# Zeros on TensorE during the first loads, and the first loads spread over three queues

## The chip, the cores and the metric

The kernel runs on one core of a Trainium2 chip. The metric is the device time of one execution in microseconds, the median of several runs. The profile is one execution of the same program under the hardware profiler.

## The reference

The kernel computes two layers of a decoder trunk over 256 tokens of 1024 features in float32. Each layer is a half-step SwiGLU FFN, a gated token-mixing block (a Mamba-2 SSD mixer and a latent attention mixer side by side), and a second half-step FFN. The start of the program, where the change lies, is the first FFN:

```
h = x
for l in range(DEPTH):
    h = h + 0.5 * swiglu(rms_norm(h, ln_ffn1[l]), ffn1_w13[l], ffn1_w2[l])
    u = rms_norm(h, ln_mix[l])
    ...
    h = h + merged @ w_o[l]
    h = h + 0.5 * swiglu(rms_norm(h, ln_ffn2[l]), ffn2_w13[l], ffn2_w2[l])

def swiglu(x, w13, w2):
    gu = x @ w13
    gate, up = gu[..., :D_FF], gu[..., D_FF:]
    return (jax.nn.silu(gate) * up) @ w2
```

D_FF is 2816.

## The kernel before

Activations lie with features on the partitions: `hT` holds x as eight tiles of 128 features x 256 tokens. Products are made in two float32r parts of each factor. `operand` (L197) makes the two parts of a feature tile: ScalarE writes the high part with the gain of the norm, VectorE the low part (L203, L204). The tile `X` then has 512 columns, high and low.

The weights stream from HBM. `plan` (L79) lists every block in the order of its use; a block is 128 x 1024 floats (512 KB), and the first four are half as wide (256 KB). `ahead` (L143) issues a block's DMA from SyncE into one of four staging buffers `st` (L148), casts its high part on ScalarE (`wh`, L151) and subtracts to get its low part on VectorE (`wl`, L152); the parts have four buffers each. `mm2` (L172) multiplies a weight tile: a matmul of 512 columns with the high weights (L177) and one of 256 columns with the low ones (L178). In the text these two are a pair; a full block is eight pairs.

In `ffn` (L378), for each of 22 feature tiles i, a gate and an up product of eight pairs each go to a PSUM tile `g` (four buffers). `halves` (L180) adds the two column halves of such a tile into `t2` (two buffers, shown as `t` in the trace): a copy on ScalarE (L181), an addition on VectorE (L182). Then comes the multiplication by the row factor `Rb` of the norm (L398), silu (L400) and the product (L401). The first FFN's `Rb` is made while the first products run: squares of x on ScalarE and their sum on VectorE (L229 to L233), a sum over partitions on TensorE (L240), `rsqrt` on VectorE (L215 to L223), a broadcast on TensorE (L255), and the copy (L260). The tables for the rotary embedding and copies of constants (`tables`, L288, with `identb` at L291) are written by VectorE between these.

`consts` (L264) starts the loads. All go out from SyncE, in this order: the norm gains `vec[0][:, :24]`, block 0, two pieces of x with block 1 behind them, two more pieces of x, blocks 2 and 3, the constants `cb`, the positions, the rest of the vectors of layer 0, the vectors of layer 1; then the further blocks.

The order of the instructions on each engine is planned when the program is built: `tile.TileContext(nc, schedule_with_timeline_sim=True)` (L904). Each engine then works through its list in that order.

Of the kernel before, what the change touches and what calls it, by code (L numbers as in the profile page):

```python
# [13 lines left out]
BF16 = mybir.dt.bfloat16  # L14
# [4 lines left out]
P = 128  # L19
L = 2  # L20
T = 256
# [14 lines left out]
XSB, ZB = 2, 1  # L36
STBUF = 4
GB, SB, HB = 4, 2, 2

# columns of the per-layer vector block  # L40
V_LN1, V_LNM, V_LN2 = 0, 8, 16
V_CW = 24
V_CB = V_CW + 96
# [9 lines left out]
V_GKP = V_GQP + 64  # L53
NV = V_GKP + 64

# columns of the constant block
C_ID, C_TRI, C_ONE, C_NEG, C_E, C_INV = 0, 128, 256, 512, 640, 672
NC_ = 704

# [1 line left out]
class Build:  # L61
# [13 lines left out]
        self.hT = self.cp.tile([P, KD, T], F32, name="hT")  # L75
        self.acc = None

# [1 line left out]
    def plan(self):  # L79
        """every weight block in the order of its use"""  # L80
        a = self.a
        self.blocks, self.used, self.split_n, self.ready = [], 0, 0, {}

        def block(key, src, n, w=P):
            self.blocks.append((key, src, n, w))

        def blocks(key, src, n=2, m=1024):
            for i in range(n):
                block(key, src[:, i * m:(i + 1) * m], m)

        def ffn(l, which):
            for i in range(KF):
                first = not self.blocks
                blocks("w13", a[f"w13_{which}"][l, i], *((4, 512) if first else ()))
            for n in range(KD):
                w2 = a[f"w2_{which}"][l, n]
                blocks("w2", w2)
                block("w2", w2[:, 2048:], 768)

        for l in range(L):  # L100
            win = a["win"][l]
            ffn(l, 1)
            block("dk", a["wdk"][l], 1024)
            blocks("gate", win[23])
            for i in range(3):
                blocks("lat", win[i])
            for kind, j in self.loop_order():
                if kind == "bc":
                    blocks("bc", win[3 + 5 * j])
                elif kind == "xs":  # L110
                    blocks("xs", win[3 + 5 * (j // 2) + 1 + j % 2])
                elif kind == "query":
                    for i in range(2):
                        block("uq", a["wuq"][l, j, :, i * 768:(i + 1) * 768], 768, 384)
                elif kind == "keyval":
                    block("ukv", a["wukv"][l, j], 1024, 512)
                elif kind == "z":
                    blocks("z", win[3 + 5 * (j // 2) + 3 + j % 2])
                elif kind == "gate":
                    blocks("gate", win[23 + j])  # L120
            for n in range(KD):
                blocks("wso", a["wso"][l, n])
                block("wmo", a["wmo"][l, n], 1024)
            for n in range(KD):
                block("wo", a["wo"][l, n], 1024)
            ffn(l, 2)
# [14 lines left out]
        return order + [("gate", n) for n in range(1, 6)] + [("z", 7), ("gate", 6), ("gate", 7)]  # L141

    def ahead(self, most=WBUF):  # L143
        """loads blocks and splits each in two float32r parts, ahead of their use"""
        while self.split_n < min(self.used + most, len(self.blocks)):
            k, src, n, w = self.blocks[self.split_n]
            st = self.stp.tile([P, 1024], F32, name="st", tag="st")[:, :n]
            self.nc.sync.dma_start(st, src)  # L148
            wh = self.whp.tile([P, 1024], F32R, name="wh", tag="wh")[:, :n]
            wl = self.wlp.tile([P, 1024], F32R, name="wl", tag="wl")[:, :n]  # L150
            self.nc.scalar.copy(wh, st)  # L151
            self.nc.vector.tensor_tensor(out=wl, in0=st, in1=wh.bitcast(F32), op=ALU.subtract)  # L152
            self.ready[self.split_n] = (k, wh.rearrange("p (k c) -> p k c", c=w), wl.rearrange("p (k c) -> p k c", c=w))
            self.split_n += 1
# [15 lines left out]
            mm(out, lhsT=wl[:, k, :], rhs=xh, start=False, stop=stop and k == nk - 1)  # L170

    def mm2(self, out, w, nk, X, x0, start, stop):  # L172
        """one load of the high weights serves both parts of X; the halves of out add up to the product"""
        wh, wl = w
        mm = self.nc.tensor.matmul
        for k in range(nk):
            mm(out, lhsT=wh[:, k, :], rhs=X[:, x0 + k, :], start=start and k == 0, stop=False)  # L177
            mm(out[:, :T], lhsT=wl[:, k, :], rhs=X[:, x0 + k, :T], start=False, stop=stop and k == nk - 1)  # L178
# [14 lines left out]
    def tmp(self, tag, shape, dt=F32, bufs=None):  # L193
        return self.tp.tile(shape, dt, name=tag, tag=tag, **({"bufs": bufs} if bufs else {}))

# [1 line left out]
    def operand(self, X, i, src, gain=None):  # L197
        hi, lo = X[:, i, :T], X[:, i, T:]
        if gain is None:
# [5 lines left out]
                                                op0=ALU.mult, op1=ALU.subtract)  # L205

    def rsqrt(self, x, n, tag):
        """1 / sqrt(x): exponent trick, one tuned Newton step, one step of third order"""
        nc = self.nc
        y = self.tmp(tag + "y", [P, n])  # L210
        t = self.tmp(tag + "t", [P, n])
        tt, stt = nc.vector.tensor_tensor, nc.vector.scalar_tensor_tensor
        c = 0.703952253
        s = math.sqrt(0.375 * c)
        nc.vector.tensor_scalar(out=y.bitcast(I32), in0=x.bitcast(I32), scalar1=-0.5, scalar2=float(0x5F1FFFF9),  # L215
                                op0=ALU.mult, op1=ALU.add)
        tt(out=t, in0=y, in1=y, op=ALU.mult)
        stt(out=t, in0=t, scalar=-1.0, in1=x, op0=ALU.mult, op1=ALU.mult)
        stt(out=y, in0=t, scalar=2.38924456, in1=y, op0=ALU.add, op1=ALU.mult)
        tt(out=t, in0=y, in1=y, op=ALU.mult)  # L220
        stt(out=t, in0=t, scalar=c * c * s, in1=x, op0=ALU.mult, op1=ALU.mult)
        stt(out=t, in0=t, scalar=-10.0 / 3.0 * s, in1=t, op0=ALU.add, op1=ALU.mult)
        self.last = stt(out=y, in0=t, scalar=5.0 * s * s, in1=y, op0=ALU.add, op1=ALU.mult).ins  # L223
        return y
# [8 lines left out]
            nc.vector.tensor_tensor(out=acc, in0=acc, in1=sq, op=ALU.add)  # L233

    def row_ms(self, acc, scale, tag):
        """mean of squares + eps, tokens on partitions: [P, 2]"""
        nc = self.nc
        ps = self.sps()
        for c in range(2):
            self.summed = nc.tensor.matmul(ps[:, c:c + 1], lhsT=acc[:, c * P:(c + 1) * P], rhs=self.ones,  # L240
                                           start=True, stop=True).ins
        return ps
# [17 lines left out]
        nc.vector.tensor_scalar(out=Rb, in0=ps[:, :T], scalar1=float(scale), scalar2=None, op0=ALU.mult)  # L260
        return Rb

# [1 line left out]
    def consts(self):  # L264
        nc, cp = self.nc, self.cp
        cb = cp.tile([P, NC_], F32, name="cb")
        pos = cp.tile([P, 2], I32, name="pos")
        self.vec = [cp.tile([P, NV], F32, name=f"vec{l}") for l in range(L)]
        load = nc.sync.dma_start
        load(self.vec[0][:, :V_CW], self.a["vec"][0, :, :V_CW])  # L270
        for n in range(0, KD, 2):
            if n in (0, 4):
                self.ahead(1 + n // 4)
            load(self.hT[:, n:n + 2, :], self.a["x"][n:n + 2].rearrange("n p t -> p n t"))
        self.ahead()
        load(cb, self.a["const"])
        load(pos, self.a["pos"])
        load(self.vec[0][:, V_CW:], self.a["vec"][0, :, V_CW:])
# [5 lines left out]
        self.ones = cp.tile([P, 1], F32, name="ones")  # L284
        nc.vector.memset(self.ones, 1.0)
        self.late = lambda: self.tables(cb, pos)

    def tables(self, cb, pos):  # L288
        nc, cp = self.nc, self.cp
# [67 lines left out]
        tt(out=b[:, :, 32:], in0=src[:, :, 0:32], in1=sg[:, :, 32:], op=ALU.mult)  # L357
        tt(out=out, in0=out, in1=b, op=ALU.add)

# [1 line left out]
    def new_X(self):  # L361
        return self.big.tile([P, KD, 2 * T], F32R, name="X", tag="X")

# [4 lines left out]
        return self.big.tile([P, 22, 2 * T], F32R, name="A", tag="A")  # L368

    def post_h(self, n, X, gain):  # L370
        """square and operand of feature tile n of the residual for the next block"""
        if n == 0:
            self.acc = self.tmp("acc", [P, T], bufs=1)
        self.operand(X, n, self.hT[:, n, :], gain[:, n:n + 1])
        self.square_into(self.acc, self.hT[:, n, :], n == 0)

# [1 line left out]
    def ffn(self, l, which, X, Xn, gain_next, late=lambda: None):  # L378
        nc = self.nc
        Rt = self.row_factor(self.acc, D, "rh")  # L380
# [34 lines left out]
            else:  # L415
                self.post_h(n, Xn(), gain_next)

# [1 line left out]
    def mix(self, l, X0, Xn, gain, gain_next):  # L419
        nc, v = self.nc, self.vec[l]  # L420
        tt, ts, stt = nc.vector.tensor_tensor, nc.vector.tensor_scalar, nc.vector.scalar_tensor_tensor
# [12 lines left out]
            self.operand(A, 16 + i, ps, v[:, o:o + 1])  # L434
            self.square_into(acc2[q], ps, i in (0, 4))

# [1 line left out]
        with self.tc.issue_after(self.last):  # L438
            ps = self.gps()[:, :T]
            self.mm(ps, self.w("dk"), KD, X0, 0, True, True)  # L440
# [27 lines left out]
            act(out=tm[:, c, :], in_=pt[:, c * P:(c + 1) * P], func=AF.Copy, scale=Rt[:, c:c + 1])  # L468
        latent(4)
        latent(5)  # L470
# [1 line left out]
        Rt2 = self.tmp("Rt2", [P, 2], bufs=1)  # L472
        tt(out=Rt2, in0=Rt, in1=Rt, op=ALU.mult)
        lm = self.tmp("lm", [P, 4], bufs=1)
# [23 lines left out]
        kpr = self.tmp("kpr", [P, 2, 64], bufs=1)  # L498
        self.rope(kpr, tm[:, :, :64], self.ropes[1])

# [1 line left out]
        x = self.tmp("dtx", [P, 2, 32], bufs=1)  # L502
        tt(out=x, in0=tm[:, :, 64:96], in1=v[:, V_DTB:V_DTB + 32].unsqueeze(1).to_broadcast([P, 2, 32]), op=ALU.add)
        e = self.tmp("dte", [P, 2, 32], bufs=1)
# [43 lines left out]
        self.accs = self.tmp("accs", [P, 2, T], bufs=1)  # L548
        for kind, j in self.loop_order():
            getattr(self, kind)(S, j)  # L550
# [1 line left out]
        tt(out=self.accs[:, 0, :], in0=self.accs[:, 0, :], in1=self.accs[:, 1, :], op=ALU.add)  # L552
        Rs = self.row_factor(self.accs[:, 0, :], 4.0 * DI, "rs")
        Rsb = self.bcast(Rs, "Rb", 0.25)
# [29 lines left out]
        S["gate", n] = gg  # L584

    def conv_pair(self, S, key, cis, out):
        """out = 2 * silu(conv) for two feature tiles"""
        nc, v = self.nc, S["v"]
        y = self.tmp("cy", [P, 2, T])
        for i, ci in enumerate(cis):  # L590
# [91 lines left out]
            nc.vector.tensor_tensor(out=self.accs, in0=self.accs, in1=z, op=ALU.add)  # L682

    def query(self, S, p):
        """queries of two heads, tokens on partitions"""
        nc, A = self.nc, S["A"]
        blocks = [self.w("uq") for _ in range(2)]
        pc = [self.gps()[:, :2 * QK] for _ in range(2)]
# [16 lines left out]
        S["query", p] = qn, qp, ss  # L705

    def keyval(self, S, p):
        """keys and values of two heads, tokens on partitions; the row factors of queries and keys"""
        nc, A = self.nc, S["A"]
        tt, act = nc.vector.tensor_tensor, nc.scalar.activation  # L710
        qn, qp, ss = S["query", p]
# [127 lines left out]


def _pack(w, nb):
    """[L, K, N] -> [L, N/(128 nb), 128, nb * K/128 * 128]: one contiguous run per partition and chunk"""
    l, k, n = w.shape
    w = w.reshape(l, k // P, P, n // (P * nb), nb, P).transpose(0, 3, 2, 4, 1, 5)
    return np.ascontiguousarray(w).reshape(l, n // (P * nb), P, nb * k)
# [63 lines left out]
```

## Time and profile before

| what | us |
|---|---|
| median of 3 runs | 1484.74 |
| lowest and highest | 1484.6, 1485.36 |
| span of the profiled execution, first to last instruction | 1480.6 |
| TensorE busy in it | 1469.6 |
| VectorE busy in it | 1119.8 |
| ScalarE busy in it | 908.6 |

Of the profiled execution only its span is known; the median of the runs lies 4.1 us above it. The busy time of TensorE counts the time in which its matmuls are under way; its waits are listed apart, by what ended them. In the rows, PE is TensorE, DVE VectorE, ACT ScalarE, SP SyncE (SPq its issuing of DMAs), POOL GpSimd.

### The profile page before, as it was taken

What the parts mean: (1) busy time and instruction counts of PE and PEld (TensorE: products, weight loads), DVE (VectorE), ACT (ScalarE), POOL (GpSimd) and SP (SyncE); (2) the same over time, 40 slices, a digit from 0 to 9 for tenths busy, and PEclk for the clock granted to TensorE, in tenths of its full rate; (3) what the DMA queues carried; (4) which work ended last, traced back from release to release, by engine and by line L of the source; (5) the groups of instructions that cost most, each with busy time, mean ns of one, the idle gap of its engine ahead of it and who ended that gap; (6) DMA issues with size and microseconds to landing.
All of it is one profiled execution on the core that took longest, in us unless ns stands there. A gap on an engine that the chain in (4) does not pass through costs nothing.

```text
span 1480.6 us, 25069 instructions
## 1 busy us (share of the span) xinstructions
PE 1469.6 (99%) x9482; PEld 1313.5 (89%) x9482; DVE 1119.8 (76%) x2089; ACT 908.6 (61%) x1736; POOL 0.2 (0%) x4
## 2 busy tenths in 40 slices
PE   7999999999999999999999999999999999999999
PEld 6888899888888998888888888998888889988888
DVE  7877679888776667777677876898887676777764
ACT  6655566887765455555455554668787654555542
POOL 0000000000000000000000000000000000000000
PEclk9999999999999999999999999999999999999999
DMA  7555655333344555556655566553434445555563
GB/s 258 189 188 172 202 178 175 134 128 122 129 142 157 185 178 187 192 191 180 194 189 193 190 184 191 175 164 123 138 126 136 142 162 188 182 185 188 190 193 116
DMA packets 73353, 252.98 MB, mean 171 GB/s; under 512 B 8337, under 2 KB 10641, under 8 KB 73233
## 3 DMA queue, kind: packets, MB, share of 16 engines
q1 hardware_dynamic: 73232, 251.39, 52.7%
q8 instruction: 74, 1.21, 0.3%
q14 instruction: 47, 0.38, 0.1%
HBM read 250.31 MB, written 1.05 MB: 170 GB/s over the span
## 4 chain that ended last, share of the span: by engine, by line
PE 99%; DMA 0%; DVE 0%; ACT 0%; issue 0%; SPq 0%; ACTq 0%; DVEq 0%
PE g L177 40%; PE g L178 20%; PE g L168 9%; PE g L169 9%; PE g L170 9%; PE g L694 2%; PE s L657 2%; PE g L718 2%; PE h L779 1%; PE h L778 1%; PE s L640 1%; PE h L802 1%; PE h L760 0%; PE s L629 0%; PE h L798 0%; DMA hT<-in_x_dram 0%
## 5 line engine op out<-in xcount | busy, mean ns | idle before, releaser
L151 ACT CAST wh<-st 128x1024 fp32r<-128x1024 f32 (+2 forms) x488 | 502.9, 1031 | 495.2 <-PE g L177 309.1
L152 DVE TENSOR_TENSOR wl<-st,wh 128x1024 fp32r<-128x1024 f32 (+2 forms) x488 | 581.5, 1192 | 258.8 <-ACT wh L151 254.5
L177 PE MATMUL g<-X,wh 128*128 128x512 f32 x928 | 329.3, 397 | 7.9 <-DVE X L204 7.5
L177 PE MATMUL g<-A,wh 128*128 128x512 f32 x938 | 327.6, 395 | 0.0
L178 PE MATMUL g<-X,wl 128*128 128x256 f32 x928 | 263.1, 284 | 0.0
L178 PE MATMUL g<-A,wl 128*128 128x256 f32 x938 | 260.6, 278 | 0.0
L177 PE MATMUL g<-oT,wh 128*128 128x512 f32 x704 | 244.5, 392 | 0.0
L168 PE MATMUL g<-X,wh 128*128 128x256 f32 x768 | 220.5, 288 | 0.0
L169 PE MATMUL g<-X,wh 128*128 128x256 f32 x768 | 219.7, 286 | 0.0
L170 PE MATMUL g<-X,wl 128*128 128x256 f32 x768 | 218.5, 285 | 0.0
L177 PEld LDWEIGHTS g<-X,wh 128*128 128x128 f32 x928 | 175.3, 189 | 47.8 <-DVE X L204 8.2
L177 PEld LDWEIGHTS g<-A,wh 128*128 128x128 f32 x938 | 175.7, 188 | 40.1
L178 PE MATMUL g<-oT,wl 128*128 128x256 f32 x704 | 196.9, 280 | 0.0
L178 PEld LDWEIGHTS g<-X,wl 128*128 128x128 f32 x928 | 176.9, 191 | 1.2 <-issue 0.3
L178 PEld LDWEIGHTS g<-A,wl 128*128 128x128 f32 x938 | 176.6, 188 | 0.4
L177 PEld LDWEIGHTS g<-oT,wh 128*128 128x128 f32 x704 | 131.6, 187 | 28.6
L168 PEld LDWEIGHTS g<-X,wh 128*128 128x128 f32 x768 | 146.3, 191 | 2.9 <-issue 1.5
L169 PEld LDWEIGHTS g<-X,wh 128*128 128x128 f32 x768 | 146.5, 191 | 2.4 <-issue 0.7
L170 PEld LDWEIGHTS g<-X,wl 128*128 128x128 f32 x768 | 146.5, 191 | 0.7 <-issue 0.2
L178 PEld LDWEIGHTS g<-oT,wl 128*128 128x128 f32 x704 | 133.0, 189 | 0.2
L170 PE MATMUL g<-oT,wl 128*128 128x256 f32 x272 | 76.8, 285 | 0.0
L169 PE MATMUL g<-oT,wh 128*128 128x256 f32 x272 | 76.7, 283 | 0.0
(288 smaller groups left out, 1849.1 us busy)
## 6 DMA issues: line engine op xcount, KB each, us to landing
st<-in_w_dram SPq DMA_DIRECT2D x238, 512.0 KB, 4.3
st<-in_win_dram SPq DMA_DIRECT2D x124, 512.0 KB, 3.8
st<-in_wso_dram SPq DMA_DIRECT2D x32, 512.0 KB, 4.2
st<-in_w_dram SPq DMA_DIRECT2D x32, 384.0 KB, 3.2
st<-in_wmo_dram SPq DMA_DIRECT2D x16, 512.0 KB, 4.1
st<-in_wo_dram SPq DMA_DIRECT2D x16, 512.0 KB, 3.5
st<-in_wuq_dram SPq DMA_DIRECT2D x16, 384.0 KB, 3.3
st<-in_wukv_dram SPq DMA_DIRECT2D x8, 512.0 KB, 3.8
```

The source lines that it names most:

```text
L151: self.nc.scalar.copy(wh, st)
L152: self.nc.vector.tensor_tensor(out=wl, in0=st, in1=wh.bitcast(F32), op=ALU.subtract)
L168: mm(out, lhsT=wh[:, k, :], rhs=xh, start=start and k == 0, stop=False)
L169: mm(out, lhsT=wh[:, k, :], rhs=xl, start=False, stop=False)
L170: mm(out, lhsT=wl[:, k, :], rhs=xh, start=False, stop=stop and k == nk - 1)
L177: mm(out, lhsT=wh[:, k, :], rhs=X[:, x0 + k, :], start=start and k == 0, stop=False)
L178: mm(out[:, :T], lhsT=wl[:, k, :], rhs=X[:, x0 + k, :T], start=False, stop=stop and k == nk - 1)
L640: nc.tensor.matmul(pbs[q][:, i * T:(i + 1) * T], lhsT=self.E[64 * q:64 * q + 64, h:h + 1].to_broadcast([64, P]), rhs=S["HL"][64 * q:64 * q ...
L657: nc.tensor.matmul(py[64 * i:64 * i + 64, q * T + c * P:(q + 1) * T], lhsT=xdt[:, c, f:f + 64], rhs=r[:, i, o:o + n], start=q == 0 and c = ...
L694: nc.tensor.matmul(pc[c], lhsT=aa, rhs=ww, start=k == 0 and i == 0, stop=k == 3 and i == 2)
L718: nc.tensor.matmul(pc[c], lhsT=aa, rhs=ww[:, k, :], start=k == 0 and i == 0, stop=k == 1 and i == 2)
L778: mm(o, lhsT=qkT[:, 0, cs], rhs=qkT[:, 1, ks], start=c == 0, stop=False)
```

## The change

Before anything else, `warm` clears a tile of 512 bf16 columns on VectorE and lets TensorE multiply it by itself twelve times, into a PSUM tile that nobody reads. The norm gains and the constants are issued from GpSimd's queue, the four pieces of x from ScalarE's; SyncE issues weight blocks alone, first block 0, then blocks 1 to 3 with nothing between them. Comments and docstrings are removed as well; that part of the diff is left out here.

```diff
+WARM = 12
...
         self.vec = [cp.tile([P, NV], F32, name=f"vec{l}") for l in range(L)]
-        load = nc.sync.dma_start
-        load(self.vec[0][:, :V_CW], self.a["vec"][0, :, :V_CW])
+        self.warm()
+        nc.gpsimd.dma_start(self.vec[0][:, :V_CW], self.a["vec"][0, :, :V_CW])
+        self.ahead(1)
         for n in range(0, KD, 2):
-            if n in (0, 4):
-                self.ahead(1 + n // 4)
-            load(self.hT[:, n:n + 2, :], self.a["x"][n:n + 2].rearrange("n p t -> p n t"))
+            nc.scalar.dma_start(self.hT[:, n:n + 2, :], self.a["x"][n:n + 2].rearrange("n p t -> p n t"))
         self.ahead()
+        load = nc.gpsimd.dma_start
         load(cb, self.a["const"])
         load(pos, self.a["pos"])
         load(self.vec[0][:, V_CW:], self.a["vec"][0, :, V_CW:])
...
+    def warm(self):
+
+        z = self.tmp("t2", [P, 2, T])[:, :, :].bitcast(BF16).rearrange("p c t -> p (c t)")[:, :512]
+        self.nc.vector.memset(z, 0.0)
+        ps = self.gps()
+        for i in range(WARM):
+            self.nc.tensor.matmul(ps, lhsT=z[:, :P], rhs=z, start=True, stop=True)
```

## Rows read from the trace of the kernel before

**Rows 1.** The page: busy time by engine, and the chain that ended last.

```profile
PE 1469.6 (99%) x9482; PEld 1313.5 (89%) x9482; DVE 1119.8 (76%) x2089; ACT 908.6 (61%) x1736; POOL 0.2 (0%) x4
...
PE 99%; DMA 0%; DVE 0%; ACT 0%; issue 0%; SPq 0%; ACTq 0%; DVEq 0%
```

**Rows 2.** Stages: length, busy time (instructions) by engine, clock, DMA share, GB/s.

```profile
100.00:1460.00 1360.00, 1360.00 (x8852) 1216.97 (x8851) 1032.31 (x1911) 842.07 (x1617) 0.00 (x0) 1.00 0.53 170
```

**Rows 3.** TensorE's waits: us in total, times, longest.

```profile
PE g L177 <- DVE X L204: 7.5, 2, 7.0
```

**Rows 4.** Timeline of TensorE, 13 to 17 us: start, duration, line, operation.

```profile
13.26 0.63 PE L177 MATMUL g<-X,wh 128*128 128x512 f32 x1
...
13.90 0.63 PE L177 MATMUL g<-X,wh 128*128 128x512 f32 x1
...
15.03 0.40 PE L177 MATMUL g<-X,wh 128*128 128x512 f32 x1
...
15.38 0.39 PE L177 MATMUL g<-X,wh 128*128 128x512 f32 x1
...
16.77 0.39 PE L177 MATMUL g<-X,wh 128*128 128x512 f32 x1
```

**Rows 5.** Stages of 2 us in the start; the last two columns are the DMA's.

```profile
2.00:4.00 2.00, 0.00 (x0) 0.00 (x0) 0.00 (x0) 0.01 (x1) 0.00 (x0) 1.00 0.62 132
...
6.00:8.00 2.00, 1.03 (x3) 0.94 (x4) 1.87 (x5) 2.00 (x6) 0.00 (x0) 1.00 0.79 254
...
12.00:14.00 2.00, 2.00 (x8) 1.73 (x8) 2.00 (x11) 1.52 (x6) 0.00 (x0) 1.00 0.99 404
```

**Rows 6.** Timeline of SyncE's issues, 0 to 14 us.

```profile
0.73 0.39 SPq L270 DMA_DIRECT2D vec<-in_vec_dram  x1
1.17 0.42 SPq L148 DMA_DIRECT2D st<-in_w_dram  x1
...
4.12 0.98 SPq L148 DMA_DIRECT2D st<-in_w_dram  x2
...
8.60 0.33 SPq L148 DMA_DIRECT2D st<-in_w_dram  x1
...
13.43 0.33 SPq L148 DMA_DIRECT2D st<-in_w_dram  x1
```

**Rows 7.** DMA issues: size, us from issue to landing.

```profile
cb<-in_const_dram SPq DMA_DIRECT2D x1, 352.0 KB, 6.7
...
vec<-in_vec_dram SPq DMA_DIRECT2D x1, 12.0 KB, 1.8
```

**Rows 8.** Timeline of ScalarE and VectorE, 5 to 19 us: in brackets idle time before, and releaser.

```profile
5.16 0.62 ACT L151 CAST wh<-st 128x512 fp32r<-128x512 f32 x1 [3.15 <-DMA st<-in_w_dram]
...
7.84 0.89 DVE L204 SCALAR_TENSOR_TENSOR X<-hT,vec,X 128x256 fp32r<-128x256 f32 x2
...
9.99 1.67 DVE L204 SCALAR_TENSOR_TENSOR X<-hT,vec,X 128x256 fp32r<-128x256 f32 x4
...
11.87 0.23 DVE L291 CAST identb<-cb 128x128 bf16<-128x128 f32 x1 [0.21 <-DMA cb<-in_const_dram]
...
12.72 0.68 DVE L152 TENSOR_TENSOR wl<-st,wh 128x512 fp32r<-128x512 f32 x1
...
15.73 1.22 DVE L152 TENSOR_TENSOR wl<-st,wh 128x1024 fp32r<-128x1024 f32 x1
...
18.32 1.05 ACT L151 CAST wh<-st 128x1024 fp32r<-128x1024 f32 x1 [1.88 <-DMA st<-in_w_dram]
```

**Rows 9.** One stage of VectorE alone: length, busy time (instructions), clock, DMA share, GB/s.

```profile
5.80:13.40 7.60, 7.26 (x21) 1.00 0.99 355
```

**Rows 10.** Timeline of VectorE and TensorE, 27 to 35 us.

```profile
27.17 1.23 DVE L152 TENSOR_TENSOR wl<-st,wh 128x1024 fp32r<-128x1024 f32 x1 [0.16 <-ACT wh L151]
28.31 0.42 DVE L260 TENSOR_SCALAR Rb<-s 128x256 f32<-128x256 f32 x1
...
34.95 0.47 PE L177 MATMUL g<-X,wh 128*128 128x512 f32 x1 [0.47 <-DVE t L182]
```

## The prediction

> **What bounds the kernel now.** I read the page first, then the stages, TensorE's waits, the first 40 us of the timeline, the DMA. The page says who sets the end: TensorE is busy for 1469.6 of 1480.6 us, and 99% of the chain that ended last is its own matmuls [rows 1]. The stages say where anything is left: between 100 and 1460 us it is busy for all 1360.00 us [rows 2]. So the whole stake is some 11 us, and all of it that this edit can touch lies in the start. TensorE waits three times in the run: 7.0 and 0.5 us for the first operands [rows 3], and 0.47 us put down to an evacuation [rows 10].
>
> The first pairs of matmuls (512 columns on the high weights, 256 on the low ones) start 0.64 us apart at 13.26 and 13.90, and 0.35 us apart at 15.03 and 15.38 [rows 4]. [...] Ten pairs (counted in the timeline, from the first one to 13.90) ran slowly: 10 x 0.29 = 2.9 us more than at full clock.
>
> That looks like what the zeros should win. The next question is whether the operands would have been there. Weight block 4 (numbered in the order of `plan`, from 0), the first of 512 KB, is split by VectorE from 15.73 to 16.95 [rows 8]; TensorE comes to block 4 at 16.77 [rows 4], after the sixteen pairs of the first four blocks, ten of them slow, and needs its low part 0.23 us later. There is no slack. Block 2's low part is ready at 13.40, though its DMA was issued at 4.12 [rows 6, 8]. In between VectorE is the busy one: 7.26 of the 7.60 us from 5.8 to 13.4, with 21 instructions [rows 9]. And the DMA engines are full from 8 us on: 0.99 of their time and 404 GB/s from 12 to 14 us [rows 5]. So in the first 17 us TensorE runs slowly, but the supply behind it is just as slow.
>
> It does not stop there. SyncE issues block 6 at 13.43, right behind the split of block 2 (four staging buffers); ScalarE has waited 1.88 us for it when it casts it at 18.32; block 10 comes the same way, cast, split at 27.17 to 28.39, and behind that split in VectorE's line stands Rb at 28.31, the row factor for which the products of the first two gate and up tiles wait; the two buffers of `t2` and the four PSUM tiles come free behind those, and TensorE waits 0.47 us at 34.95 [rows 6, 8, 10]. TensorE restarts there on a chain that goes back to the split of block 2. From 35 us on nothing waits, so the shift at 34.95 is the shift of the end.
>
> **The change part by part.** *Twelve matmuls on zeros.* A memset of 512 columns on VectorE is not in the trace; it costs more than nothing, and less than the 1.22 us of a full split [rows 8]. I take 0.6, half of that row since it writes half the columns, on an engine that has nothing to do until the first block lands. Twelve matmuls of 512 columns at half clock are two thirds of 0.64 each, 0.43, 5.1 us in all [rows 4]. From about 1.4 to 6.6 us they lie inside the 7.0 us that TensorE waits anyway [rows 3]. If the first operand came 0.5 us sooner, they would cost 0.1. The PSUM tile and the buffer of `t2` that they hold come round again only at the third and fourth use. In the likeliest case the clock is then up by the first or second real pair: 2.9 us are offered.
>
> *x on ScalarE's queue.* Four issues at SyncE's 0.49 us each are 2.0 in all [rows 6]. ScalarE has been idle for 3.15 us before its first cast, with the activation table already loaded [rows 8]: covered, 1.2 us to spare; without that cover all 2.0 would fall on the first cast. SyncE loses these and the vector's issue: block 0 goes out at 0.73 and not at 1.17, 0.44 us earlier, and blocks 2 and 3 some 2.4 us earlier.
>
> *Constants on GpSimd's queue.* The trace has no transfer of that queue. The nearest row is the same vector on SyncE, 1.8 us to landing [rows 7]; the largest constant there is cb with 6.7. Issued at 0.5 us it lands between 2.3 and 7.2; needed at 5.9, when the first operand is made. It is far nearer to the first row in size, so I take 3, which costs nothing; the far end would cost 1.3 us of the first operand. Blocks 4 and 5 no longer queue behind constants: 4 goes out at about 6.5, when the split of block 0 frees a buffer, and not at 8.60 [rows 6].
>
> *What the supply gains.* The same bytes must land before block 4 is there. What the queues can give back is time in which the engines were not full: 132 GB/s from 2 to 4 us and 254 from 6 to 8, against 404 [rows 5]. (404-132) x 2 + (404-254) x 2 us are 0.84 MB, 2.1 us at 404. So the supply moves by 0 to 2.1 us. [...] I take the 0.44 us of the earlier first issue and a quarter of the 2.1: 0.9.
>
> [...]
>
> *Sum.* At block 4 TensorE has no slack of its own, so of the 2.9 us it keeps what the supply gives: 0.9. At 34.95 the chain from block 2 moves by the same 0.9, and the 0.47 us wait stays. The rest is waited away. Span 1480.6 - 0.9 = 1479.7; the median of the runs, 1484.74, lies 4.1 above the span, and this overhead stays: 1483.8 us.
>
> **The rivals.** *Faster: TensorE sets the pace.* The order on each engine is planned at build time on a simulated timeline (the last lines of the kernel); with other landings VectorE may take the splits ahead of the squares and tables, some 3 us of the 7.26. If blocks 2 to 4 and Rb come more than 2 us sooner, TensorE keeps 2.9 + 0.5 + 0.47 and 0.4 of an earlier start: 4.3 us, 1480.4. For: tables and squares are not urgent. Against: Rb needs the squares, and the 4.9 us from the issue of block 6 to its cast [rows 6, 8] are not VectorE's.
>
> *Little worse: the constants overtake.* By their shapes they are 128 rows of 704, 352 and 376 floats, 0.73 MB, now behind x and the first blocks, and would share the engines with them. 0.73 MB at 404 GB/s [rows 5] is 1.8 us for the last tiles of x. VectorE makes these at 9.99 to 11.66 [rows 8]; less the 0.9 gained, that is 0.9 slower: 1485.6. For: a third queue doesn't wait for the other two. Against: the copy of cb itself is put in line only after the vector's.
>
> *Slower: VectorE stands in line for a constant.* In the trace it waits 0.21 us for cb before identb at 11.87 [rows 8]. If the plan puts identb ahead of the operands of x, believing that cb is early, and cb lands as late as now, everything behind it on VectorE waits: from the second pair of operands on, at 7.84 [rows 8], that is 4.0 us; 1488.7 less 0.9, 1487.8. It decides from 3 us of waiting. For: the constants' landing on the new queue is unknown. Against: they start 4 us earlier. [...]
>
> *The zeros don't raise the clock in time.* Then the first pairs stay slow, and the supply's 0.9 is kept only in part, by an earlier first pair: 1484.3.
>
> **How the numbers follow.** The supply-bound case 0.50, its own range 1482.5 to 1484.8; TensorE's pace 0.22; the constants overtake 0.14; VectorE in line 0.08; no clock 0.06. 0.2% is 3.0 us, about what a measurement of this kernel can tell from no change. Only the second case and a small tail of the first are faster by more: 0.23. Slower by more is the case in line: 0.08. All else, 0.69, is within. The range goes down to the middle of the fast case, which I see between 1479.5 and 1481.7, 1480.6, and leaves out 0.11 there; above it ends at 1486.4, 0.8 beyond the overtaking's point for a landing of the constants that costs as much again, and leaves out the 0.08 in line.
>
> **What the changed profile would show.** Right: 512-column zeros from about 1.4 us; real pairs 0.35 us apart by 8 us; new waits of TensorE between 8 and 17 us, for the later operands and splits, together about 2 to 3 us; first matmul of block 4 near 16; restart near 34.0. The faster case: first matmul of block 4 before 14.5 and no wait near 30. The overtaking: cb landed before the last x. In line: identb, or what stands for it, with an idle of several us before it. I would be wrong by a step that I can't see: a stall after 40 us through a new order, or time outside the span for the third queue.

## The result, and the profile after

| | before | after |
|---|---|---|
| median of 4 runs, us | 1485.05 | 1492.49 |
| lowest and highest, us | 1484.6, 1485.63 | 1490.5, 1493.13 |
| the profiled execution, us (its span) | (1480.6) | 1493.13 (1491.3) |

The ratio is 1.0051, with a 95% interval of 1.0039 to 1.0063: the kernel became slower, by 7.4 us, and the time is above the whole of the predicted range. The page of the changed kernel, busy times, chain and the new queue:

```profile
PE 1478.2 (99%) x9494; PEld 1316.4 (88%) x9494; DVE 1120.7 (75%) x2090; ACT 909.1 (61%) x1736; POOL 3.0 (0%) x9
...
q0 software_dynamic: 272, 0.75, 0.1%
...
PE 98%; DMA 1%; ACT 0%; DVE 0%; issue 0%
```

TensorE's chain still sets the end [rows 1]. Its waits (us in total, times, longest) say where it stopped:

```profile
PE g L178 <- DVE t L183: 4.5, 1, 4.5
PE g L178 <- DVE X L205: 3.8, 2, 3.4
PE g L295 <- DVE ef L498: 1.2, 1, 1.2
```

The wait for the first operands is in good part filled with zeros now [rows 3]. The new one is the first row: one wait of 4.5 us for an evacuation, where it was 0.47 [rows 10]. The stages show both ends of the start, and the rest (length; busy PE, PEld, DVE, ACT, POOL; clock, DMA share, GB/s):

```profile
4.80:8.20 3.40, 0.90 (x4) 0.20 (x2) 1.29 (x2) 1.36 (x3) 0.00 (x0) 1.00 0.98 361
8.20:15.00 6.80, 5.50 (x16) 4.33 (x17) 5.76 (x19) 4.98 (x13) 0.00 (x0) 0.50 1.00 360
...
38.90:45.70 6.80, 4.46 (x14) 3.81 (x15) 5.89 (x17) 4.14 (x13) 0.00 (x0) 0.50 0.25 91
...
100.00:1470.00 1370.00, 1370.00 (x8904) 1225.00 (x8903) 1039.14 (x1923) 848.29 (x1626) 0.00 (x0) 1.00 0.53 170
```

From 100 us on nothing has changed: TensorE is busy all the time [rows 2]. In the start it runs at half the clock (granted 0.50) in two stretches, each of which begins in a pause of TensorE: 8.2 to 15.0, in the 3.38 us up to 9.09, although the zeros came first, and 38.9 to 45.7, in the 4.52 us up to 41.24. Timeline of the changed kernel, first 20 us (start, duration, engine, line, operation, idle time before):

```profile
1.19 4.51 PE L295 MATMUL g<-t 128*128 128x512 bf16 x12 [1.19 <-DVE ef L498]
1.25 0.67 POOL L271 DMA_DIRECT2D vec<-in_vec_dram  x1 [0.81 <-POOLq L909]
...
4.73 0.37 ACTq L274 DMA_DIRECT2D hT<-in_x_dram  x1
...
8.01 0.91 ACT L204 ACTIVATE X<-hT,vec 128x256 fp32r<-128x256 f32 x2 [0.44 <-DMA vec<-in_vec_dram]
...
9.09 0.80 PE L178 MATMUL g<-X,wh 128*128 128x512 f32 x1 [3.38 <-DVE X L205]
...
9.92 0.23 DVE L300 CAST identb<-cb 128x128 bf16<-128x128 f32 x1 [0.48 <-DMA cb<-in_const_dram]
...
15.28 0.91 ACT L204 ACTIVATE X<-hT,vec 128x256 fp32r<-128x256 f32 x2 [0.80 <-DMA hT<-in_x_dram]
...
17.59 1.23 DVE L153 TENSOR_TENSOR wl<-st,wh 128x1024 fp32r<-128x1024 f32 x1
```

The zeros end at 5.70. ScalarE, though, waits for the norm gains until 8.01, so the first real matmul starts at 9.09. The fourth pair of x tiles becomes an operand only at 15.28, and block 4 is split at 17.59, 1.9 us later than at 15.73 [rows 8]. The DMA issues tell why (engine, size, us from issue to landing):

```profile
vec<-in_vec_dram POOLq DMA_DIRECT2D x1, 12.0 KB, 6.7
...
cb<-in_const_dram POOLq DMA_DIRECT2D x1, 352.0 KB, 8.0
...
hT<-in_x_dram ACTq DMA_DIRECT2D x1, 256.0 KB, 10.5
```

The 12 KB of the gains took 6.7 us on GpSimd's queue and 1.8 on SyncE's [rows 7]. cb was there at 9.9; x's pieces landed at 5.34, 7.79, 12.41 and 15.25 (before at 5.80, 6.52, 8.52 and 9.22, by the DMA's landings in both traces).

Then the stretch of the new wait, from the same timeline:

```profile
34.25 0.61 PE L256 MATMUL s<-cb,rhy 128*128 128x128 f32 x4
35.62 0.42 DVE L261 TENSOR_SCALAR Rb<-s 128x256 f32<-128x256 f32 x1
36.07 1.29 DVE L407 TENSOR_TENSOR t<-t,Rb 128x512 f32<-128x512 f32 x2
36.44 0.28 PE L179 MATMUL g<-X,wl 128*128 128x256 f32 x1
36.64 1.04 ACT L152 CAST wh<-st 128x1024 fp32r<-128x1024 f32 x1 [2.20 <-PE g L178]
37.70 1.28 ACT L409 ACT_TABLE_LOAD   x1
39.00 0.72 ACT L409 ACTIVATE ta<-t 128x256 f32<-128x256 f32 x2
40.68 0.75 DVE L183 TENSOR_TENSOR t<-t,g 128x256 f32<-128x256 f32 x2
41.24 0.77 PE L178 MATMUL g<-X,wh 128*128 128x512 f32 x1 [4.52 <-DVE t L183]
```

Two things had to be there before ScalarE's silu at 39.00. One is the product of a gate tile with the row factor: the broadcast on TensorE at 34.25, the copy Rb, and the product from 36.07 on, whose first half was done by 36.8. The other is silu's table, loaded at 37.70 behind the cast at 36.64, and this cast waited 2.20 us for TensorE to free a weight buffer. The second came last. The profile's own chain to the restart goes through it and not through Rb (start, length, what; left out are short pieces, and the steps from silu at 39.00 to the evacuation):

```profile
36.38 0.24 PE g L178
...
36.64 1.04 ACT wh L152
...
37.70 1.28 ACT L409
...
41.24 0.77 PE g L178
```

TensorE's own work ran out at 36.72: only six pairs stood behind the broadcast in its list, and the cast waited for the last of them. Before, the copy Rb was made at 28.31 and the restart came at 34.95 [rows 10].

**Where the time went.** A second profile of the kernel before (1485.2 us, span 1483.1) has the same steps, a little later than the first. There the cast ahead of silu's table is released at 29.14, when TensorE still has sixteen pairs to do:

```profile
27.09 0.61 PE L255 MATMUL s<-cb,rhy 128*128 128x128 f32 x4
...
29.14 1.05 ACT L151 CAST wh<-st 128x1024 fp32r<-128x1024 f32 x1 [2.21 <-PE g L177]
...
30.21 1.28 ACT L400 ACT_TABLE_LOAD   x1
...
35.25 0.47 PE L177 MATMUL g<-X,wh 128*128 128x512 f32 x1 [0.47 <-DVE t L182]
```

Against it the span after is 8.2 us longer. The restart is 6.0 us later (41.24 - 35.25): TensorE's work ran out 2.0 us later (36.72 against 34.77), which is the share of the operands' and blocks' supply, and the wait is 4.0 us longer. Behind the restart seven pairs at half clock take 0.64 us and not 0.35, 2.0 us. The other three runs of the changed kernel have a mean clock of 0.997 against 0.995 in the profiled one, so this last stretch seems not to be in all of them.

### The profile page after: what moved, and what is told of

Same layout as the page of the kernel before. It is cut to its first block, busy times and chain, and to the rows that moved or that the text cites. A ratio compares the mean times of both kernels' runs of the same rounds, so it can differ in the third digit from the quotient of the medians.

```text
span 1491.3 us, 25097 instructions
## 1 busy us (share of the span) xinstructions
PE 1478.2 (99%) x9494; PEld 1316.4 (88%) x9494; DVE 1120.7 (75%) x2090; ACT 909.1 (61%) x1736; POOL 3.0 (0%) x9
## 4 chain that ended last, share of the span: by engine, by line
PE 98%; DMA 1%; ACT 0%; DVE 0%; issue 0%
PE g L178 40%; PE g L179 20%; PE g L169 9%; PE g L170 9%; PE g L171 9%; PE g L703 2%; PE s L666 2%; PE g L727 2%; PE h L788 1%; PE h L787 1%; PE s L649 1%; DMA hT<-in_x_dram 1%; PE h L811 1%; PE h L769 0%; PE s L638 0%; PE h L807 0%
```

## The experiments

Line numbers from here on are those of the changed kernel unless said otherwise. Each kernel was timed against the kernel before on the same chip; times are medians.

**x first.** Do the four issues of x cost time because one of them stood behind the first cast, at 4.73?

```diff
-        self.ahead(1)
         for n in range(0, KD, 2):
             nc.scalar.dma_start(self.hT[:, n:n + 2, :], ...)
+        self.ahead(1)
         self.ahead()
```

> The changed kernel with its four x issues written ahead of block 0, so that all four stand at the head of ScalarE's list and none behind the first cast. Theory A (the fourth issue, at 4.73 us behind the cast, makes the last piece of x land at 15.25 instead of 9.22, and the row factor and the restart of TensorE follow it): the last piece is issued by 2.7 us and lands at 11 to 12.5, the restart moves from 41.2 to 37 to 38.5, the time from 1492.5 to 1488 to 1490. Theory B (the constants on GpSimd's queue share the engines and the norm gains land at 7.98): the same bytes move, so the restart stays within 1 us of 41.2 and the time at 1491.5 to 1493.

1492.44 us, 1.0051 [1.0038, 1.0063]: nothing came back. All four went out in one go, and the last operand was as late (ScalarE's timeline):

```profile
0.74 2.49 ACTq L273 DMA_DIRECT2D hT<-in_x_dram  x4
...
15.26 0.91 ACT L204 ACTIVATE X<-hT,vec 128x256 fp32r<-128x256 f32 x2 [1.10 <-DMA hT<-in_x_dram]
```

The late issue is not the cause; whether the other loads hold x up is the next question.

**Constants back on SyncE.**

```diff
-        nc.gpsimd.dma_start(self.vec[0][:, :V_CW], self.a["vec"][0, :, :V_CW])
+        nc.sync.dma_start(self.vec[0][:, :V_CW], self.a["vec"][0, :, :V_CW])
...
-        load = nc.gpsimd.dma_start
+        load = nc.sync.dma_start
```

> The changed kernel with the norm gains and the constants issued from SyncE, first and last as in the kernel before; zeros and x on ScalarE stay (the planner now puts all four x issues ahead of the cast). Theory A alone (late fourth issue): x lands no earlier than in the run with x first, so the time is the same as there, 1488 to 1490. Theory B (constants): x lands by 9.5, the gains by 3 us, the first operand is ready by 6.5, the restart is at 34 to 35.5 and the time 1484 to 1485.5.

1489.84 us, 1.0032 [1.0021, 1.0042]: a third of the loss is gone, most of it is not. All of x had landed by 10.24, 5 us sooner, and the broadcast moved from 34.25 to 31.33, yet TensorE stands as long as in the changed kernel (its timeline):

```profile
31.33 0.60 PE L256 MATMUL s<-cb,rhy 128*128 128x128 f32 x4
...
38.20 0.49 PE L178 MATMUL g<-X,wh 128*128 128x512 f32 x1 [4.53 <-DVE t L183]
```

A supply that comes sooner takes nothing off this wait. So it isn't the supply's. Neither theory had this: the time lies in the range of the first, but x did land sooner.

**Loads moved, without zeros.** The edit is `- self.warm()`.

> The changed kernel without the memset and the twelve zero matmuls; the loads stay on three queues. Theories A and B (the loads are the loss): still slow, 1491 to 1494, since the zeros' full clock was over before the first real matmul. Theory C (the zeros bring the clock's fall): the loss is smaller by more than 2 us, 1490 or less.

1493.43 us, 1.0052 [1.0038, 1.0065]: the whole loss. The wait was 4.5 us.

**Zeros alone.** The kernel before, with `WARM = 12` and `self.warm()` ahead of its loads, which stay on SyncE.

> The kernel before with the memset and the twelve zero matmuls, and no other edit; order of loads as before. Supply-bound theory of the prediction: restart at 34.5 to 35, time within 0.7 us of before, 1484.4 to 1485.7, the first pairs at full clock or not. Theory Z (what TensorE's clock costs at the start is worth its 2.9 us when the loads come as before): restart near 32, 1482 to 1482.5.

1487.62 us, 1.0024 [1.0016, 1.0033]: slower by 3.6 us, though no transfer had moved. This was a miss for every theory so far, and the trace shows the same wait again (timeline of TensorE and ScalarE):

```profile
29.40 0.61 PE L256 MATMUL s<-cb,rhy 128*128 128x128 f32 x4
...
31.10 1.06 ACT L152 CAST wh<-st 128x1024 fp32r<-128x1024 f32 x1 [1.77 <-PE g L178]
...
37.20 0.47 PE L178 MATMUL g<-X,wh 128*128 128x512 f32 x1 [3.24 <-DVE t L183]
```

**A new theory: the place of the broadcast.** What these kernels have in common stands in the engines' lists of instructions, which are fixed when the program is built. TensorE has 64 pairs to work on until both buffers of `t2` and all four PSUM tiles are full (blocks 0 to 9). The theory: those pairs that stand behind the broadcast, at 0.35 us each, cover the way from it through VectorE and ScalarE to the restart, so a broadcast that stands later in the list leaves less cover. Counted in the lists of the programs, with times from the traces:

| kernel | pairs ahead of the broadcast | pairs behind it | broadcast to restart, us | casts ahead of silu's table load | last of these casts to restart, us | wait measured, us |
|---|---|---|---|---|---|---|
| before | 43 | 21 | 8.2 | 12 | 6.1 | 0.47 |
| after | 58 | 6 | 7.0 | 14 | 4.6 | 4.52 |
| zeros alone | 52 | 12 | 7.8 | 13 | 6.1 | 3.24 |
| loads, no zeros | 57 | 7 | 7.6 | 14 | 4.6 | 4.53 |
| constants on SyncE | 59 | 5 | 6.9 | 14 | 4.6 | 4.53 |
| x first | 60 | 4 | 6.3 | 14 | 4.6 | 4.52 |

(before: its second profile.) For the theory speaks that the cover goes from 21 pairs to 4, some 6 us, while the time from the broadcast to the restart changes by 1.9 us at most. Against it as the whole account speak the four kernels with 7 to 4 pairs: their waits are the same, 4.52 to 4.53.

The casts in ScalarE's list tell more. The weight parts have four buffers, so the twelfth cast can begin when TensorE is through with 48 of the 64 pairs, the thirteenth after 56 and the fourteenth after all 64; in these traces the last cast ahead of silu begins within 0.05 us of the end of that pair's high matmul. Behind it TensorE has 16, 8 or no pairs left, that is 5.6, 2.8 or 0 us of work, and the wait is what remains of 6.1, 6.1 and 4.6 us: 0.5, 3.3, 4.6. So in these kernels the restart hangs on the cast, and with fourteen casts TensorE waits for the end of its own work. The planner moved the broadcast and the casts together. In the changed kernel silu could have begun 2.2 us sooner without the fourteenth cast ahead of it (36.8, when the product was there, and not 39.00); that is an estimate, since no kernel here moves a cast by itself.

The next kernels were made for the theory: an edge holds the broadcast to another place, and nothing else is edited. The planner orders the rest of each list anew around it.

**Broadcast late in the kernel before**, with an edge that puts it behind the products of gate tile 3:

```diff
+            self.low = mm(out[:, :T], lhsT=wl[:, k, :], ...).ins         # in mm2
...
+            self.spread = nc.tensor.matmul(ps[:, c * P:(c + 1) * P], ...).ins   # in bcast
...
+        spread = self.spread                                             # in ffn
...
+                    if first and (i, g) == (3, 0):
+                        self.tc.add_manual_dep(spread, self.low.name, mybir.DependencyInfo(
+                            mybir.DependencyClass.NoSync, mybir.DependencyReason.DATA), reason="late")
```

> The kernel before with one edit: the second half of the first row factor's broadcast on TensorE is ordered behind the 56th pair of matmuls (before: behind the 43rd; in the changed kernel it is behind the 58th). No zeros, loads as before. Theory P (the changed kernel loses its time because the planner puts this broadcast later in TensorE's list, so that too little work is left to cover the chain from it to the evacuation of PSUM): broadcast at 31.3 us, restart of TensorE 8 us later at 38.5 to 39.5, a wait of 4 to 5 us instead of 0.47, and if the clock falls in it 1 to 2 us more: 1489 to 1492. Theory L (the loads, late x and constants, are the loss): nothing changes, 1484.5 to 1486.

1488.34 us, 1.0026 [1.0016, 1.0036]: 3.6 us slower with neither zeros nor another queue. The planner left one of the broadcast's halves at 43 pairs and put the other behind 56 (L255 is the kernel before's number for it):

```profile
27.30 0.38 PE L255 MATMUL s<-cb,rhy 128*128 128x128 f32 x2
...
31.81 0.39 PE L255 MATMUL s<-cb,rhy 128*128 128x128 f32 x2
...
38.05 0.47 PE L177 MATMUL g<-X,wh 128*128 128x512 f32 x1 [3.08 <-DVE t L182]
```

The wait is some 1 us shorter than expected, and the time just below the expected range. This profile is of one of the two quickest of nine executions (1485.77 us); its span, 1483.7, is to be held against the first profile of the kernel before (1480.6), which has the same pace of pairs (348 matmuls from 100 to 160 us in both). An edge on the broadcast alone makes the loss. But with it the planner put thirteen casts ahead of silu's table, not twelve (the last begins at 31.89, 6.2 us ahead of the restart), so this run doesn't tell the broadcast's place from the casts'.

**Broadcast early in the changed kernel.** The edge is the other way round: products of tile (3, 0) come behind the broadcast.

```diff
+        spread = self.spread
...
                 for g in range(2):
+                    if first and (i, g) == (3, 0):
+                        order.enter_context(self.tc.issue_after(spread))
```

> The changed kernel with one edit: the matmuls of the fourth feature tile (pair 49 on) are ordered behind the broadcast of the first row factor, which so stands behind pair 48 and not 58. Zeros and the three queues as in the changed kernel, the last x still late. Theory P: the broadcast runs at about 31 instead of 34.25, the restart comes at 38 to 39 instead of 41.2, the wait is 1 to 2.5 us, and the clock doesn't fall a second time: 1487 to 1489.5. Theory L: the row factor is late because x is, so the edge only moves the wait: 1491 to 1493.

1488.52 us, 1.0023 [1.0014, 1.0032]. The broadcast stands behind 48 pairs, and the wait has gone from 4.52 to 0.60 us:

```profile
30.82 0.71 PE L256 MATMUL s<-cb,rhy 128*128 128x128 f32 x4
...
37.78 0.47 PE L178 MATMUL g<-X,wh 128*128 128x512 f32 x1 [0.60 <-DVE t L183]
```

That gives back 4.0 us of the 7.4. Twelve casts stand ahead of silu's table again, and silu, at 33.76, follows the product with Rb and no cast. The second stretch at half the clock is gone from this trace as well (the pairs behind 37.78 start 0.35 us apart, and the mean clock is 0.997, not 0.995), which is of a quick execution again (1485.75 us). What is left, 3.4 us, should be the loads', which the next two kernels test.

**The same, and the gains alone back on SyncE** (`nc.gpsimd` to `nc.sync` in the line of `self.vec[0]`):

> As the run before in this batch, but only the norm gains go back to SyncE, as its first issue; the constants stay on GpSimd's queue. Theory V (of GpSimd's queue, the late gains are the cost, landing at 7.98): first operand by 7, 1485 to 1487. Theory W (the constants' traffic ahead of x is the cost): the last x still lands after 12, the row sum and the restart stay as late as with the edge alone, 1487.5 to 1489.

1485.97 us, 1.0005 [0.9996, 1.0014]. Another 0.18% is gone, 2.7 us, with one issue of 12 KB. The gains landed 2.5 us after their issue, and the first operand is no longer held by them. VectorE is held by something else now, so TensorE's first real matmul came only 0.75 us sooner (8.54 against 9.29 with the edge alone). But the last piece of x landed at 11.84 and not at 15.48. Its issue had moved ahead of the first cast, as in "x first", where that alone changed nothing (15.24); why x comes sooner here stays open. A DMA row, and a row of VectorE's timeline:

```profile
vec<-in_vec_dram SPq DMA_DIRECT2D x1, 12.0 KB, 2.5
...
7.55 0.23 DVE L300 CAST identb<-cb 128x128 bf16<-128x128 f32 x1 [6.39 <-DMA cb<-in_const_dram]
```

**The same, and all constants back on SyncE** (the diff of the second experiment and the edge):

> The changed kernel with the broadcast ordered ahead of pair 49 (as in the run of the changed kernel with that edge, 1488.5), and the norm gains and constants issued from SyncE, first and last; zeros and x on ScalarE stay. Theory Q (with the broadcast's place held, what is left of the loss is GpSimd's queue: late gains and constants that share the engines with x): broadcast at 28.5, restart at 35.5 to 36.5, no second fall of the clock, 1484.5 to 1486.5. Rival (x on ScalarE's queue or the zeros cost the rest): 1488 to 1489.

1485.39 us, 1.0000 [0.9991, 1.0009]. The step from the kernel above is within the intervals: the big constants cost little beside the gains.

**Zeros alone, with the broadcast held early.** The loads stand as before; the edge is at tile (2, 1), and tile 1 comes behind the sum over partitions (`if i == 1:` in place of `if i == 1 and not first:`).

> The kernel before with the zeros (as in the run with zeros only), and the row factor's sum ordered ahead of pair 17 and its broadcast ahead of pair 41 (with zeros only they stand behind 24 and 52, before behind 16 and 43). Theory P: no wait of over 1 us near 35, restart at 34 to 35.5, no fall of the clock there: 1482.5 to 1485. Rival (the zeros themselves cost, by the clock that falls after them or by the PSUM tile and the buffer that they hold): 1487 to 1488 as with zeros only.

1483.92 us, 0.9996 [0.9988, 1.0005]: the 3.6 us that zeros alone had cost are back. The broadcast is at 26.10 behind 40 pairs, eleven casts stand ahead of silu's table, and no wait for an evacuation is left (waits):

```profile
PE g L178 <- DVE X L205: 2.8, 3, 1.2
...
PE g L179 <- DVE wl L153: 1.1, 1, 1.1
PE s L241 <- DVE acc L234: 0.6, 1, 0.6
```

What replaces it are waits for operands, for a split and for the row sum: the supply. (The wait of 1.2 us for `ef` is the zeros' own.)

**The edges alone**, on the kernel before:

> The kernel before with the two ordering edges alone (row sum ahead of pair 17, broadcast ahead of pair 41), no zeros. It tells what the zeros are worth once the broadcast's place is held: zeros with these edges gave 1483.9. Supply-bound theory of the prediction (TensorE keeps none of its own 2.9 us): 1483.9 to 1484.7, so the zeros are worth under 0.8 us. Rival (the full clock counts in full): 1486 or more.

1483.4 us, 0.9992 [0.9984, 1.0001]. Beside it the zeros of the kernel above are worth nothing that can be measured, although there they did raise the clock in time: it is granted in full from 4.88 us on, and the first two real pairs start 0.46 us apart, not 0.81. TensorE still came to block 4 at 17.56 us with them and at 17.30 without.

**Constants held behind block 4**, on top of the zeros with the edges: the four issues of the constants get an edge behind the issue of block 4.

> Zeros and both edges as in that run (1483.9), all loads from SyncE, with the constants issued behind block 4 instead of ahead of it. If the supply of blocks 2 to 4 in the first 17 us is what holds TensorE, block 4 lands 1 to 2 us sooner and VectorE has no table work ahead of the splits: 1482 to 1483.5. If VectorE's work alone holds it, or the tables then stand in the way of the row factor, no change: 1483.5 to 1484.5.

1484.15 us, 0.9997 [0.9988, 1.0005]: no change, although block 4 landed at 12.23 and not at 14.33. TensorE waited 1.1 us for the row sum in place of the splits (waits, L245 and L238 are that kernel's numbers for the sum):

```profile
PE g L182 <- DVE X L209: 2.4, 3, 1.1
PE s L245 <- DVE acc L238: 1.1, 1, 1.1
```

VectorE, busy for all 9.00 us from 8 to 17 us here, is next in line behind the transfers.

**The kernel before once more**, with a profile, was run for the sums above:

> The kernel before, unchanged, with a profile. The first profile's span, 1480.6, and the 1.8 us that other runs show outside the span give 1482.4, below the median of 1485.2. If a fall of the clock in the start is what most executions of it have and the first profile had not, this profile shows a stretch at half clock after 30 us and a span near 1483.4; if not, the span is 1480.6 again and the difference lies outside it.

1485.2 us, span 1483.1.

No version is shown to be faster than the kernel before: the best, the edges alone, has 1.0001 as its upper bound.

## Why the prediction was wrong

**The step that failed** is in the sum: "At 34.95 the chain from block 2 moves by the same 0.9, and the 0.47 us wait stays." The wait was 4.52 us, and the restart came at 41.24. The step took the order of the instructions as given, and with it the work that TensorE still had while silu was made ready. That order is a result of the planner, and the planner's input had changed. The prediction knew of it: the faster rival and the one with VectorE in line rest on it, and "a stall after 40 us through a new order" is among the last things that it names. But for the wait at 34.95 it priced only the way down, 0.47 us.

The path was misread too. TensorE's restart did not go back to block 2 by way of Rb: in the second profile of the kernel before, the product with Rb was there by 29.3 us, and silu began at 31.51, behind its table load at 30.21 and the twelfth cast at 29.14, which TensorE's own 48th pair released. So the price of a new order could be read from ScalarE's list: each cast of a full block that moves ahead of silu takes eight pairs, 2.8 us, off the cover. Two moved.

What is shown is that the order makes the loss: an edge on the broadcast alone makes a slow kernel out of the kernel before (+3.6 us), and one the other way round takes 4.0 us off the changed one. That the wait goes by the casts is read from the traces, by the chain and by the equal waits at 4 to 7 pairs behind the broadcast; no run moves casts and broadcast separately. Why the planner moves them, for twelve matmuls on zeros too, stays open; only the lists were read.

**The gains on GpSimd's queue.** "I take 3, which costs nothing": they landed at 7.98. The bounds were 2.3 and 7.2, and the value was taken by size; the 12 KB took 6.7 us, as long as cb's 352 KB had taken on SyncE [rows 7], while cb behind them took 8.0. The issue was also later than the 0.5 us that I took, 1.25. The first real matmul came at 9.09, 2.2 us later than in the second profile of the kernel before (6.92). With the place held, moving this one load back takes 2.7 us off (1.0023 to 1.0005), but TensorE's first matmul is only 0.75 us sooner by it, and the last piece of x 3.6; which of the two makes how much stays open.

**The rival that the constants overtake** had its sign in the profile, cb landed ahead of the last two pieces of x (9.9 against 12.41 and 15.25), and its size was too small. I priced it by bytes, 1.8 us; the last piece landed 6.0 us later (15.25 against 9.22). It was not the chain that decided: with the constants back on SyncE x was there by 10.24, and the restart still 3 us late. But it turned the sum's term for the supply round: block 4 landed 0.7 us sooner (13.43 against 14.12), near the 0.9 that I took, and TensorE's work still ran out 2.0 us later. The quarter of the 2.1 us in that 0.9 was my estimate, and no run shows it by itself. The size of x's rows, 1 KB, explains little of the 6.0 us: by the packets in the two traces 1 KB took 46 ns (median) on SyncE's queue before and on ScalarE's after, and 4 KB took 159 and 166. By the landings in the two traces nothing was gained in all: blocks 0 to 2 landed 0.4 to 0.9 us sooner, the first piece of x 0.5 and cb 2.0, while the other pieces of x landed 1.3, 3.9 and 6.0 us later and the gains 5.4.

**VectorE in line for a constant** did not happen in the changed kernel (0.48 us at 9.92). It did happen with the gains alone on SyncE, 6.39 us at 7.55. It held the first operand there: TensorE's first real matmul came at 8.54, and at 7.46 with all constants on SyncE. The end hardly shows it, 1.0005 against 1.0000.

**The zeros.** They cost what was said, 0.43 us each at first, from 1.19 to 5.70, inside the time that TensorE waits anyway; the memset took 0.27 us, not 0.6. The clock rose while they ran (the first nine start 0.42 us apart, the last three 0.22). The next part, "the clock is then up by the first or second real pair", failed: the operands came 3.4 us after the last zero, and from 8.2 to 15.0 the granted clock is 0.50. That stretch begins 2.5 us into the wait for operands; the second, from 38.9 on, begins 2.2 us into the wait for an evacuation. For the kernel before, the slow first pairs are read from their steps alone, since the clock column shows 1.00 there [rows 4, 5]: 0.64 us, the same as between the pairs that start at 11.96 and 12.60 in the changed kernel, where 0.50 is granted.

**What held.** "So in the first 17 us TensorE runs slowly, but the supply behind it is just as slow": with the place of the broadcast held, the kernel before is no faster with the zeros than without (0.9996 against 0.9992, within both intervals). With them the clock was up from 4.88 us on, so what the zeros offer was there, and it was waited away. A block 4 that lands 2.1 us sooner only hands the wait to VectorE's sum. And from 100 us on nothing moved.

**The overhead of 4.1 us** outside the span was misread, without effect on the result: where one execution has both numbers, 1.7 to 2.2 us lie outside the span, before and after. By that the first profile was one of the quicker executions (some 1482.7).

In all, by the ratios at 1485 us, each of them known to some 1.3 to 1.8 us: the order, held by the edge on the broadcast, 4.2 us (1.0051 to 1.0023), the gains on GpSimd's queue 2.7 (to 1.0005), and the remaining 0.7 for the other constants, no more than the intervals. The traces allow a second count that leaves out how fast the rest of an execution goes, by the start of TensorE's hundredth pair: 47.2 and 47.7 us in the two profiles before, 55.7 after, 50.0 with the edge, 48.2 with the gains back as well, 48.1 with all constants back. By it the order is worth 5.7 us (the wait 3.9, and 2.2 behind it, most of which is the second stretch at half the clock; less 0.5, since TensorE's work ran out at 37.18 there), the gains 1.8 and the other constants 0.1. The two counts put the three in the same order.

## What to carry to other kernels

Where a planner orders the instructions at build time, an edit far from a chain can move that chain: compare the lists of all engines before trusting any duration, and look first at the waits that are almost covered, since their cover is what a new order takes away. Ask of such a wait what it really follows: here a cast that itself waited for TensorE. An explicit edge (here a broadcast ahead of a product tile) holds the order, so that other edits can be compared. Before a small load that everything waits for goes to another queue, look at when it lands there: here 12 KB took 6.7 us as the first issue of GpSimd's queue and 2.5 as SyncE's, and moving them back gave 2.7 us.

## What the runs showed of the hardware

The pace of the pairs differs between executions at a granted clock of 1.00. Two stretches of the second profile of the kernel before (columns as in the stages above):

```profile
40.00:100.00 60.00, 60.00 (x342) 52.05 (x341) 49.13 (x95) 34.97 (x66) 0.00 (x0) 1.00 0.57 188
100.00:160.00 60.00, 60.00 (x343) 52.19 (x342) 43.77 (x69) 32.65 (x56) 0.00 (x0) 1.00 0.58 181
```

The first profile has 348 matmuls in each of these stretches, busy all the time as well. Eleven more in 120 us, at 0.175 us each, are 1.9 of the 2.5 us between the two spans. Runs of this one program lie between 1482.0 and 1485.9, and the cause is open; single executions are no measure of the few us that this case is about.

A load of 12 KB from GpSimd's queue took 6.7 us beside the first loads of the other two queues; as SyncE's first issue it took 1.8 us, and 2.5 with x's first piece issued from ScalarE at the same time.
